# The last 16 pairs of a gated channel mixer as Strassen's seven products, their weight sums made by adding DMA transfers

## The chip, the cores and the metric

The kernel runs on one core of a Trainium2 chip. The metric is the device time of one execution in microseconds (us); the kernel before has a median of 989.22 us over three runs (987.55 to 991.62). The core's engines are TensorE (PE, with its weight loads as PEld), VectorE (DVE), ScalarE (ACT), GpSimd (POOL) and SyncE (SP). SP issues the weight loads; POOL and ACT issue some transfers as well. Tiles in on-chip memory have 128 partitions; matmuls write to PSUM banks of 128 x 512 float32.

## The reference

One block of a streaming encoder, for 512 tokens of 1024 channels. Two token mixers run side by side on the normalised input (a gated delta rule of eight heads, and a convolution with a layer norm); sigmoid gates merge them, an output projection `w_out` adds the result to the input, and then comes the part that the change is about:

```python
h2 = rmsnorm(x, norm2_w[l])
f_gate, f_up = jnp.split(h2 @ ffn_w_gate_up[l], 2, axis=-1)
x = x + (jax.nn.silu(f_gate) * f_up) @ ffn_w_down[l]
return rmsnorm(x, norm_f_w)
```

The hidden width is 2816, that is 22 tiles of 128 columns for the gate and 22 for the up half: 22 pairs.

## The kernel before

Every matmul on weights is done in three terms. `unit` (L92 to L105) loads a weight tile `raw` of 128 x 1024 float32 on SP's queue (512 KB; or two halves of 256 KB), ACT copies it, rounded, to `whi` (L102), and DVE subtracts for the rest, `wlo` (L104); `raw`, `whi` and `wlo` have three buffers each. `split3` (L107 to L113) then issues three matmuls, high weights by high inputs, high by low, low by high. So all these matmuls have the line L113, and the "weight split" of the text is ACT's L102 with DVE's L104.

**Channel mixer** (L873 to L902). For each pair f two column tiles are made, gate and up, each of 8 row blocks by 3 terms: 24 matmuls of 512 columns (all tokens), 48 in a pair. The weights stand still, the normalised tokens `hh`, `hl` move. ACT makes the silu of the gate, DVE the product `fm` (L888). For f below 11, `sums(f)` runs on POOL beside that (L861 to L868): it loads 1 MB of down weights (`wst`), makes four combinations in place (L864 to L867) and stores them (`wsum`, 1 MB). In the second half DVE makes the combinations of the hidden tiles (L898 to L902). `xsplit` (L853, L854) makes high and low parts of an operand, `fh` and `fl`.

**Down product** (from L936). It is already a form of Strassen's method: the hidden tiles are taken as 11 blocks, tokens and columns in halves, and seven products p1 to p7 take the place of eight. `two` runs two products at a time over k = 0 to 10, four banks of PSUM, 12 matmuls of 512 columns for each k; its weights are halves `wd` of the loaded matrix and the stored sums `wsum`. Between them DVE and POOL add the products to the residual `y1` (called A in the trace). p3 comes last (L991 to L1016): six weight tiles, the last three of them first for token block 0, and then for token block 1 in two parts of 256 columns.

**The end.** `norm_f` (L911 to L922) takes each finished part: ACT squares and sums, POOL adds the sums (L796) and raises to the power -1/2 (L798), POOL multiplies the first half of the columns by the norm's weights (L916, to `o0`), ACT scales it (L918), DVE does the second half in one operation (L920, to `o1`), and both halves are stored.

**What sets the order.** The functions are written in order, and a recording layer with a scheduler puts each engine's instructions in a row; each engine works through its row in order and waits for semaphores. So an instruction that waits holds all that stand behind it on its engine. POOL's row also holds the layer norm's sums (L575, `sacc`), for whose end TensorE has a matmul by ones (L580), and the powers of norm 2. In late heads the work is cut into small steps, counted by `count[0]`.

## Time and profile before

| | |
|---|---|
| median of 3 runs | 989.22 us (987.55 to 991.62) |
| the profiled execution's own time | 987.57 us |
| its span (first to last instruction) | 985.8 us |
| matmuls / weight loads | 4775 / 4775 |
| ACT weight copies, 128 x 1024 | 167, mean 1057 ns |
| DVE weight splits, 128 x 1024 | 167, mean 1285 ns |
| loads of gate and up tiles | 44 of 512 KB, 3.4 us to landing |
| DMA traffic | 138.5 MB, mean 140 GB/s |
| read from HBM / written | 119.52 MB / 18.10 MB |

By the chain and the timeline the stages lie as follows: the layer norm's sums on POOL start at 501.7 us, the output products of the two mixers last to 575.6, `w_out` with norm 2 to 635.9, the pairs of the channel mixer to 864.2, the down product to 977.9, the last stores to 985.8.

How rows are read: a row of the timeline has start, duration, engine, line, operation, what is written and read, shape, and how often; in brackets the idle time of the engine before it and what ended that. A row of a group has the busy time and the mean ns of one, then the idle time ahead of the group's instructions. A row of the waits has the total, how many and the longest. A row of the issues has the engine's queue (SPq, POOLq), how many, KB each and the us to landing. Records of matmuls overlap, so that the pace of matmuls is read from their starts.

### The profile page before, as it was taken

The numbers are of one execution on the slowest core, as the hardware profiler recorded it, in microseconds if no ns is written. First come the engines' busy times: TensorE is split into PE (matmuls) and PEld (weight loads), VectorE is DVE, ScalarE is ACT, GpSimd is POOL, SyncE is SP. The second block draws the span as 40 slices with busy tenths as digits, with TensorE's granted clock in tenths as the row PEclk, the third lists the DMA queues.
The fourth block names the chain that finished last, engine by engine and source line by source line (L and its number), as shares of the span: only waits on it lengthen the run. The fifth ranks groups of instructions, "written<-read, shape, count | busy, mean of one in ns | idle before, by whom it ended". The sixth has DMA issues, their size and how long they took to land.

```text
span 985.8 us, 13439 instructions
## 1 busy us (share of the span) xinstructions
PE 955.7 (97%) x4775; PEld 785.7 (80%) x4775; DVE 669.8 (68%) x1044; ACT 513.6 (52%) x1062; POOL 255.1 (26%) x410
## 2 busy tenths in 40 slices
PE   7999999999999999999999999999999999999995
PEld 5688878878787778888878888888888888888784
DVE  4899888888787669889578544542434464469953
ACT  6689777777767664543446323432223322256543
POOL 0314543343243240000050001243534432001412
PEclk9999999999999999999999999999999999999997
DMA  8233421413212122234744432556565565256462
GB/s 317 88 119 120 120 91 41 127 68 98 77 65 88 65 87 69 97 124 144 272 137 137 146 115 65 166 192 246 186 242 206 203 211 184 92 168 196 160 207 86
DMA packets 48291, 138.50 MB, mean 140 GB/s; under 512 B 7472, under 2 KB 9424, under 8 KB 45408
## 3 DMA queue, kind: packets, MB, share of 16 engines
q1 hardware_dynamic: 44016, 112.36, 34.4%
q0 software_dynamic: 3488, 24.17, 6.9%
q10 hardware_dynamic: 720, 1.11, 0.3%
q8 instruction: 37, 0.61, 0.3%
q14 instruction: 30, 0.25, 0.1%
HBM read 119.52 MB, written 18.10 MB: 140 GB/s over the span
## 4 chain that ended last, share of the span: by engine, by line
PE 84%; ACT 5%; DVE 4%; POOL 4%; issue 2%; DMA 1%; SPq 0%; POOLq 0%; ACTq 0%; DVEq 0%
PE mm L113 64%; PE w L113 11%; DVE wlo L104 1%; POOL Un L350 1%; ACT cp L355 1%; ACT Un L349 1%; PE st L477 1%; PE b L415 1%; PE b L421 1%; PE st L483 1%; POOL ytm L376 1%; PE st L489 1%; PE g L346 1%; DMA raw<-in_win_dram 1%; PE st L478 1%
## 5 line engine op out<-in xcount | busy, mean ns | idle before, releaser
L102 ACT ACTIVATE whi<-raw 128x1024 fp32r<-128x1024 f32 x167 | 176.1, 1057 | 327.1 <-PE mm L113 191.9
L113 PE MATMUL mm<-hh,whi 128*128 128x512 f32 x816 | 325.9, 400 | 0.0
L113 PE MATMUL mm<-hl,whi 128*128 128x512 f32 x816 | 321.9, 395 | 2.3 <-POOL hl L229 1.6
L113 PE MATMUL mm<-hh,wlo 128*128 128x512 f32 x816 | 322.3, 395 | 0.0
L104 DVE TENSOR_TENSOR wlo<-raw,whi 128x1024 fp32r<-128x1024 f32 x167 | 214.5, 1285 | 114.7 <-ACT whi L102 114.1
L545 DVE SCALAR_TENSOR_TENSOR cps<-c,c31w,cps 128x512 f32<-128x512 f32 x240 | 180.0, 750 | 4.9 <-ACT cps L543 1.0
L113 PEld LDWEIGHTS mm<-hl,whi 128*128 128x128 f32 x816 | 153.5, 188 | 33.0 <-POOL hl L229 2.9
L113 PEld LDWEIGHTS mm<-hh,wlo 128*128 128x128 f32 x816 | 153.4, 188 | 30.1
L113 PEld LDWEIGHTS mm<-hh,whi 128*128 128x128 f32 x816 | 153.5, 188 | 29.2 <-ACT hh L228 0.2
L888 DVE TENSOR_TENSOR fm<-mm,fsg 128x512 f32<-128x512 f32 x21 | 14.5, 692 | 67.0 <-PE mm L113 67.0
L300 DVE SCALAR_TENSOR_TENSOR acc<-mm,c4w,acc 128x509 f32<-128x509 f32 (+2 forms) x72 | 52.6, 738 | 1.5 <-ACT acc L297 1.2
L376 POOL TENSOR_TENSOR ytm<-U,y 128x60 f32<-128x60 f32 (+14 forms) x120 | 36.9, 307 | 60.6 <-DMA U<-sc 51.9
L113 PE MATMUL mm<-yh,whi 128*128 128x512 f32 x128 | 50.6, 396 | 0.0
L113 PE MATMUL mm<-yh,wlo 128*128 128x512 f32 x128 | 49.8, 389 | 0.0
L113 PE MATMUL mm<-yl,whi 128*128 128x512 f32 x128 | 49.8, 389 | 0.0
L113 PE MATMUL w<-whi,fh 128*128 128x512 f32 (+1 forms) x115 | 45.3, 395 | 2.8 <-ACT whi L102 2.8
L113 PE MATMUL w<-wlo,fh 128*128 128x512 f32 (+1 forms) x115 | 45.6, 397 | 2.4 <-DVE wlo L104 2.4
L113 PE MATMUL w<-whi,fl 128*128 128x512 f32 (+1 forms) x115 | 45.0, 393 | 0.0
L378 POOL TENSOR_TENSOR y<-y,ytm 128x60 f32<-128x60 f32 (+14 forms) x120 | 34.9, 291 | 9.4
L511 POOL TENSOR_TENSOR ss<-ss,half 128x4 f32<-128x4 f32 x8 | 8.1, 1014 | 109.5 <-DVE ss L509 109.5
L796 POOL TENSOR_SCALAR ss<-ss 128x1 f32<-128x1 f32 x17 | 5.7, 338 | 117.9 <-ACT sg L794 105.3
L864 POOL TENSOR_TENSOR wst<-wst 128x512 f32<-128x512 f32 x11 | 15.2, 1386 | 62.7 <-DMA wst<-in_wdn_dram 62.7
(288 smaller groups left out, 1489.1 us busy)
## 6 DMA issues: line engine op xcount, KB each, us to landing
raw<-in_win_dram SPq DMA_DIRECT2D x61, 512.0 KB, 3.3
raw<-in_wgu_dram SPq DMA_DIRECT2D x44, 512.0 KB, 3.4
wst<-in_wdn_dram POOLq DMA_DIRECT2D x11, 1024.0 KB, 5.7
wsum<-wst POOLq DMA_DIRECT2D x11, 1024.0 KB, 4.7
raw<-wsum SPq DMA_DIRECT2D x44, 256.0 KB, 3.2
raw<-in_wdn_dram SPq DMA_DIRECT2D x33, 256.0 KB, 2.9
A<-in_x_dram SPq DMA_DIRECT2D x8, 512.0 KB, 6.3
U<-sc SPq DMA_DIRECT2D x64, 64.0 KB, 2.3
```

The lines of the kernel that those rows point to most:

```text
L102: marked(S.activation(hi[:, 0:n], raw[:, 0:n], AF.Copy), "unit")
L104: marked(V.tensor_tensor(out=lo[:, 0:n], in0=raw[:, 0:n], in1=hi[:, 0:n].bitcast(F32), op=ALU.subtract), "unit")
L113: marked(PE.matmul(ps, l, r, start=first and i == 0, stop=last and i == 2))
L300: marked(V.scalar_tensor_tensor(out=acc[:, s:], in0=ps[:, :T - s], scalar=c4w[:, j, k:k + 1], in1=acc[:, s:], op0=ALU.mult, op1=ALU.add))
L346: PE.matmul(ps[:, n, :], kT[:, n, :], kT[:, n, :], start=True, stop=True)
L349: S.activation(Un[:, n, :], ps[:, n, :], AF.Copy, scale=nb2[:, n:n + 1])
L350: G.tensor_tensor(out=Un, in0=Un, in1=DT, op=ALU.mult)
L376: G.tensor_tensor(out=tm[:, :, 0:w], in0=U[:, k, :, k + 1:], in1=y[:, :, k:k + 1].broadcast_to([P, NT, w]), op=ALU.mult)
L378: last[0] = G.tensor_tensor(out=y[:, :, k + 1:], in0=y[:, :, k + 1:], in1=tm[:, :, 0:w], op=ALU.add)
L545: V.scalar_tensor_tensor(out=acc, in0=c[:, k:k + T], scalar=c31w[:, i, k:k + 1], in1=acc, op0=ALU.mult, op1=ALU.add)
L864: G.tensor_tensor(out=b11, in0=b12, in1=b11, op=ALU.subtract)
L888: V.tensor_tensor(out=fm, in0=pu, in1=sg, op=ALU.mult)
```

## The change

The first six pairs (f = 0 to 5) stay as they are. For each of the last 16, gate and up tile, tokens and rows in halves are taken as a 2 x 2 block product with seven products (`pair`): `hprod` is one of them, 4 row blocks by 3 terms, 12 matmuls of 256 columns (half of the tokens), 84 in a pair. DVE, ACT and PSUM banks combine them to the gate and the up half, and the silu follows. The token sides T1 to T4 of the products are made once, from sums of quarters of `hh` + `hl`. The weight sides are three and a half weight tiles in a pair: a tile `w` as it is, `w46` with half a tile as it is and a sum, `w37` with two sums, `w5` with one.

The sums s1 to s4 of the weights, 16 tiles of 256 KB each, 64 in all, lie in DRAM. `feed_one` makes one: SP copies a part of the gate and up matrix into the tile (behind the weight load just issued, on the same queue), and POOL then issues a transfer that adds another part or another sum (waiting until the copy and, where it takes another sum, that one have landed). One tile is made with each weight tile that is loaded while `start_feed` is set: from count 335 of the heads on, through the output products, the first half of `w_out`, and f = 1 to 9.

The rest follows from the places taken. The down weights' sums are called `dsums`, are written as additions only (signs are taken into the adds of the products) and run on POOL behind every odd pair instead of every early one. The combinations of the hidden tiles and the adds that make p3's operands go from DVE to POOL in part. The residual is stored to DRAM in norm 2 by ACT's queue and loaded back as `y2`, 4 x 512 KB, on SP between the raw halves of the first down product. The load of the last norm's weights moves to the start of the down product. `set_2` to `set_4` are made two k later. At the end, the adds of p4 and p2 and the squares are written between the first k of p3, and POOL's multiply by the norm's weights stays for two of four token blocks; the other two are done by DVE with stores at once.

The core of the diff:

```diff
+        aps = ap if isinstance(ap, tuple) else (ap,)
+        n = T * len(aps) if isinstance(ap, tuple) else 1024
+        raw, hi, lo = ((pool or wp).tile([P, n if pool else 1024], t, name=x)[:, 0:n]
+                       for t, x in ((F32, "raw"), (F32R, "whi"), (F32R, "wlo")))
+        for i, p in enumerate(aps):
+            loads.append(nc.sync.dma_start(raw[:, i * T:(i + 1) * T] if len(aps) > 1 else raw, p))
+        if start_feed[0] and feed:
+            feed_one(last[0])
...
+    FK, F0 = FF // 2, 6
+    sums = {n: dram.tile([FF - F0, P, T], F32, name=n, bufs=1) for n in ("s1", "s2", "s3", "s4")}
+    gu = {n: a["wgu"][r * FF + F0:(r + 1) * FF][:, :, c * T:(c + 1) * T]
+          for n, r, c in (("A11", 0, 0), ("A12", 0, 1), ("A21", 1, 0), ("A22", 1, 1))}
+    feed = [("s1", 0)] + [w for p in range(FF - F0) for w in (("s3", p), ("s2", p), ("s1", p + 1), ("s4", p))]
+    feed = [(*w, *{"s1": ("A21", gu["A22"]), "s3": ("A11", gu["A21"]), "s2": ("A11", sums["s1"]),
+                   "s4": ("A12", sums["s2"])}[w[0]]) for w in feed if w[1] < FF - F0]
+    fed = []
+    def feed_one(behind_):
+        n, p, m, other = feed.pop(0)
+        with tc.issue_after(loads[-1].ins):
+            nc.sync.dma_start(sums[n][p], gu[m][p])
+        with tc.issue_after((fed[-1] if fed else behind_).ins):
+            fed.append(nc.gpsimd.dma_start(sums[n][p], other[p], accum_op=ALU.add, max_dma_last_dim=2048))
...
+        start_feed[0] = count[0] >= 335
...
+            start_feed[0] = not hf
...
+            nc.scalar.dma_start(ysp[n], y1[:, n, :])
...
-        G.tensor_tensor(out=b11, in0=b12, in1=b11, op=ALU.subtract)
-        G.tensor_tensor(out=b12, in0=b22, in1=b12, op=ALU.subtract)
-        G.tensor_tensor(out=b22, in0=b22, in1=b11, op=ALU.subtract)
-        G.tensor_tensor(out=b21, in0=b22, in1=b21, op=ALU.subtract)
+        tt(b22, b12, b22, ALU.add, G)
+        tt(b12, b11, b12, ALU.add, G)
+        tt(b11, b22, b11, ALU.add, G)
+        tt(b21, b11, b21, ALU.add, G)
...
+    def pair(f):
+        z = [bank() for _ in range(4)] if f % 2 == 0 else [bank(), bank2(), bank2(), bank2()]
+        s = lambda n: sums[n][f - F0]
+        w = unit(a["wgu"][f])
+        w46 = unit((a["wgu"][FF + f][:, T:], s("s2")))
+        hprod(z[0][:, t1], w, 0, B11)
+        hprod(z[1][:, t1], w, 1, B21)
+        hprod(z[2][:, t1], w46, 0, T4)
+        w37 = unit((s("s4"), s("s3")))
+        hprod(z[0][:, t2], w46, 1, T2)
+        cw = fq.tile([P, T], F32, name="cw", bufs=2)
+        S.copy(out=cw[:, t1], in_=z[0][:, t1])
+        u = fq.tile([P, TH], F32, name="cu")
+        tt(u, cw[:, t1], z[0][:, t2], ALU.add)
+        hprod(z[1][:, t2], w37, 0, B22)
+        w5 = unit((s("s1"),))
+        hprod(z[3][:, t1], w37, 1, T3)
+        v = fq.tile([P, TH], F32, name="cv2")
+        tt(v, u, z[3][:, t1], ALU.add)
+        if f == F0:
+            xsplit(*T1, b11)
+        hprod(z[2][:, t2], w5, 0, T1)
+        tt(cw[:, t2], u, z[2][:, t2], ALU.add)
+        fm = hidden()
+        tt(fm.rearrange("p (i t) -> p i t", i=2), z[2].rearrange("p (i t) -> p i t", i=2),
+           v.rearrange("p (a t) -> p a t", a=1).broadcast_to([P, 2, TH]), ALU.add)
+        tt(cw, cw, z[1], ALU.add)
+        S.activation(cw, cw, AF.Silu)
+        V.scalar_tensor_tensor(out=fm, in0=fm, scalar=-1.0, in1=cw, op0=ALU.mult, op1=ALU.mult)
...
+        if f % 2 and f // 2 < FK:
+            dsums(f // 2)
+        if f < 2 * F0:
+            operands(f - F0)
+        operands(f)
...
+            if also:
+                with tc.issue_after(loads[-1].ins):
+                    nc.sync.dma_start(*also.pop(0))
             for i in range(2):
                 prods(w, i, xs[k], i, banks[2 * i:2 * i + 2], k == 0, k == FK - 1)
-            then(k)
-
-    def next_set(dst, src):
-        def then(k):
-            dst.append(xset())
-            xsplit(*dst[k], src(k))
-        return then
+            if k > 1:
+                then(k - 2)
...
+        if k < 2:
+            add(2 + k, c1, p4[k])
+            squares(0, 2 + k, c1)
+            squares(1, 2 + k, c2, True)
+        elif k < 4:
+            add(k - 2, c1, p2[k - 2])
+            for cs, eng in ((c1, nc.scalar), (c2, nc.sync)):
+                scaled_out(k, cs, eng)
+            first_half(k - 2)
```

In this diff `tt` is a tensor_tensor on DVE or, with G, on POOL; `bank` and `bank2` give PSUM tiles.

**POOL at the layer norm's sums.** POOL's row before, from the last `ss` of the heads' norms on: `sacc` is the sum over the eight channel tiles, `acc4` the tiles.

```order
L511 TENSOR_TENSOR ss_3642<-ss_3642,half4_83 128x4
L746 DMA nw2_5407<-in_n2w_dram 128x1024
L575 TENSOR_TENSOR sacc_5113<-sacc_5113,acc4_5117 128x512
L575 TENSOR_TENSOR sacc_5113<-sacc_5113,acc4_5121 128x512
L575 TENSOR_TENSOR sacc_5113<-sacc_5113,acc4_5125 128x512
L575 TENSOR_TENSOR sacc_5113<-sacc_5113,acc4_5129 128x512
L575 TENSOR_TENSOR sacc_5113<-sacc_5113,acc4_5133 128x512
L575 TENSOR_TENSOR sacc_5113<-sacc_5113,acc4_5137 128x512
L575 TENSOR_TENSOR sacc_5113<-sacc_5113,acc4_5141 128x512
```

POOL's row of the changed kernel at the same place; `s1` to `s4` are the sums' tiles in DRAM, and a DMA row with `s3<-in_wgu_dram` or `s2<-s1` is the adding transfer's issue.

```order
L160 DMA s3_126<-in_wgu_dram 128x512
L160 DMA s2_125<-s1_124 128x512
L160 DMA s1_124<-in_wgu_dram 128x512
L160 DMA s4_127<-s2_125 128x512
L601 TENSOR_TENSOR sacc_5157<-sacc_5157,acc4_5161 128x512
L601 TENSOR_TENSOR sacc_5157<-sacc_5157,acc4_5165 128x512
L601 TENSOR_TENSOR sacc_5157<-sacc_5157,acc4_5169 128x512
L601 TENSOR_TENSOR sacc_5157<-sacc_5157,acc4_5173 128x512
L160 DMA s3_126<-in_wgu_dram 128x512
L601 TENSOR_TENSOR sacc_5157<-sacc_5157,acc4_5177 128x512
L601 TENSOR_TENSOR sacc_5157<-sacc_5157,acc4_5181 128x512
L601 TENSOR_TENSOR sacc_5157<-sacc_5157,acc4_5185 128x512
```

The seven adds, which stood behind one another, now stand behind the feed's issues, and one issue stands between the fourth and the fifth. (L601 is L575 of before.)

**DVE in the pairs.** DVE's row before, from the second half of f = 10 to the combinations of f = 11, the first late pair; `fm` is a hidden tile, `fl` the low part of an operand, `s1` a combination.

```order
L104 TENSOR_TENSOR wlo_7076<-raw_7072,whi_7074 128x1024
L854 TENSOR_TENSOR fl_6995<-fm_6985,fh_6994 128x256
L104 TENSOR_TENSOR wlo_7108<-raw_7104,whi_7106 128x1024
L888 TENSOR_TENSOR fm_7062<-mm_6999,fsg_7030 128x512
L898 TENSOR_TENSOR s1_7064<-fm_6215,fm_7062 128x256
L104 TENSOR_TENSOR wlo_7148<-raw_7144,whi_7146 128x1024
L854 TENSOR_TENSOR fl_6225<-s1_7064,fh_6224 128x256
L901 TENSOR_TENSOR fm_6215<-fm_6215 128x256
L902 TENSOR_TENSOR fm_6215<-s1_7064,fm_6215 128x256
```

DVE's row of the changed kernel through one Strassen pair (f = 10); `cw`, `cu`, `cv2` are the partial sums out of the banks `w`, L1005 the product with the silu.

```order
L108 TENSOR_TENSOR wlo_7436<-raw_7434,whi_7435 128x1024
L889 TENSOR_TENSOR cu_7370<-cw_7368,w_7296 128x256
L889 TENSOR_TENSOR cv2_7402<-cu_7370,w_7299 128x256
L108 TENSOR_TENSOR wlo_7442<-raw_7440,whi_7441 128x1024
L889 TENSOR_TENSOR cw_7368<-cu_7370,w_7298 128x256
L889 TENSOR_TENSOR fm_7417<-w_7298,cv2_7402 128x512
L889 TENSOR_TENSOR cw_7368<-cw_7368,w_7297 128x512
L108 TENSOR_TENSOR wlo_7485<-raw_7483,whi_7484 128x1024
L1005 SCALAR_TENSOR_TENSOR fm_7417<-fm_7417,cw_7368 128x512
L108 TENSOR_TENSOR wlo_7520<-raw_7518,whi_7519 128x512
L886 TENSOR_TENSOR fl_7427<-fm_7417,fh_7426 128x256
L886 TENSOR_TENSOR fl_7564<-fm_6684,fh_7563 128x256
```

Where a late pair had two splits, `fm` and four short operations, a pair now has four splits (one of half size), five sums out of PSUM, the product and two low parts.

**DVE at the end of the down product.** DVE's row before, with p3's weight splits; A is the residual, `o1` the finished second halves.

```order
L104 TENSOR_TENSOR wlo_8638<-raw_8633,whi_8636 128x1024
L925 TENSOR_TENSOR A_5409<-A_5409,w_8337 128x512
L104 TENSOR_TENSOR wlo_8645<-raw_8640,whi_8643 128x1024
L925 TENSOR_TENSOR A_5409<-A_5409,w_8335 128x512
L925 TENSOR_TENSOR A_5409<-A_5409,w_8336 128x512
L925 TENSOR_TENSOR A_5409<-A_5409,w_8338 128x512
L104 TENSOR_TENSOR wlo_8652<-raw_8647,whi_8650 128x1024
L920 SCALAR_TENSOR_TENSOR o1_8603<-A_5409,ss3_7794,nfw_6152 128x512
L920 SCALAR_TENSOR_TENSOR o1_8622<-A_5409,ss3_7794,nfw_6152 128x512
L104 TENSOR_TENSOR wlo_8659<-raw_8654,whi_8657 128x1024
```

DVE's row of the changed kernel at the same place; `y2` is the reloaded residual.

```order
L108 TENSOR_TENSOR wlo_9748<-raw_9746,whi_9747 128x1024
L889 TENSOR_TENSOR y2_8935<-y2_8935,w_9490 128x512
L889 TENSOR_TENSOR y2_8935<-y2_8935,w_9491 128x512
L108 TENSOR_TENSOR wlo_9755<-raw_9753,whi_9754 128x1024
L889 TENSOR_TENSOR y2_8935<-y2_8935,w_9493 128x512
L1036 SCALAR_TENSOR_TENSOR o1_9815<-y2_8935,ss3_8936,nfw_8933 128x512
L1036 SCALAR_TENSOR_TENSOR o1_9818<-y2_8935,ss3_8936,nfw_8933 128x512
L108 TENSOR_TENSOR wlo_9762<-raw_9760,whi_9761 128x1024
L108 TENSOR_TENSOR wlo_9769<-raw_9767,whi_9768 128x1024
L1036 SCALAR_TENSOR_TENSOR o1_9832<-y2_8935,ss3_8936,nfw_8933 128x512
L108 TENSOR_TENSOR wlo_9776<-raw_9774,whi_9775 128x512
L1036 SCALAR_TENSOR_TENSOR o1_9835<-y2_8935,ss3_8936,nfw_8933 128x512
```

In both, two `o1` stand ahead of the fourth split of p3. Before, they belonged to two token blocks (2 and 3), so that the second waited for the second root factor; now both belong to block 2, and the two of block 3 follow, one behind the fifth split and one behind the sixth.

More of the change, by code (lines that the diff above doesn't have):

```diff
@@ L574, in ln_mean @@
                 S.activation(sq2, cv[i], AF.Square)
[L575 removed]
+                last[0] = G.tensor_tensor(out=vacc, in0=vacc, in1=sq2, op=ALU.add)
         return vacc
@@ L760, in block_kernel @@
         V.tensor_tensor(out=ml[j], in0=mb, in1=mh[j].bitcast(F32), op=ALU.subtract)
+    ysp = [dram.tile([P, D], F32, name="ysp", bufs=NT) for _ in range(NT)]
     def tok_mm(wname, kts, xh, xl, post, between):
@@ new lines, in block_kernel @@
+    kl, kh = slice(0, KH), slice(KH, KD)
+    xb = []
+    for i, (ks, ts, eng) in enumerate(((kl, t1, V), (kl, t2, V), (kh, t2, V), (kh, t1, G))):
+        xb.append(fx.tile([P, KH, TH], F32, name="xb%d" % i))
+        tt(xb[i], hh[:, ks, ts].bitcast(F32), hl[:, ks, ts].bitcast(F32), ALU.add, eng)
+    b11, b12, b22, b21 = xb
+    tt(b11, b11, b12, ALU.subtract)
+    last[0] = tt(b12, b22, b12, ALU.subtract, G)
+    tt(b22, b22, b11, ALU.add)
+    tt(b21, b22, b21, ALU.subtract)
+    T2, T3, T4 = ([fq.tile([P, KH, TH], F32R, name="%s%d" % (n, i)) for n in ("th", "tl")] for i in range(3))
@@ L905, in block_kernel @@
+    fxd = False
+    for f in range(F0, FF):
+        pair(f)
+        if not fxd:
+            fxs.close()
+            ff = ctx.enter_context(tc.tile_pool(name="ff", bufs=FK))
+            fxd = True
+        if f % 2 and f // 2 < FK:
+            dsums(f // 2)
+        if f < 2 * F0:
+            operands(f - F0)
+        operands(f)
+    fqs.close()
     hps.close()
     dp = ctx.enter_context(tc.tile_pool(name="dp", bufs=2, side="right"))
+    nfw = dp.tile([P, D], F32, name="nfw", bufs=1)
@@ L1015, in block_kernel @@
         add(1, cs, ps)
-        norm_f(4 if c else 1, 1, cs)
+        squares(4 if c else 1, 1, cs, c)
+        if not c:
+            out(0)
+    out(1)
 def _layout(i):
```

188 lines of the change are left out of this document (102 added, 86 removed).

## The prediction

> **What bounds the kernel now.** I read the busy shares first, then the chain that ended last, then what TensorE waited for, and then single stretches of the timeline. The page's busy row and its chain row:
>
> ```profile
> PE 955.7 (97%) x4775; PEld 785.7 (80%) x4775; DVE 669.8 (68%) x1044; ACT 513.6 (52%) x1062; POOL 255.1 (26%) x410
> PE 84%; ACT 5%; DVE 4%; POOL 4%; issue 2%; DMA 1%; SPq 0%; POOLq 0%; ACTq 0%; DVEq 0%
> ```
>
> TensorE is busy for 97% of the span, and the chain lies on it for 84%. What is to be had are fewer or shorter matmuls, and its few waits:
>
> ```profile
> PE w L113 <- DVE wlo L104: 2.9, 4, 1.4
> PE w L113 <- ACT whi L102: 2.8, 1, 2.8
> ```
>
> These (total us, times, longest us) are in the down product and at its end. The channel mixer has none: the chain of waits holds one piece of 1007 matmuls.
>
> ```profile
> 635.92 228.28 PE mm L113 x1007
> ```
>
> 228.28 / 1007 = 0.2267 us for a matmul of 512 columns, and 48 of them make a pair of column tiles: 10.88 us.
>
> **Sixteen pairs as seven products: −13.5.** A pair becomes 7 × 12 = 84 matmuls of 256 columns. The kernel has 42 of that form in a row after norm 2; the first and the last:
>
> ```profile
> 623.10 0.28 PE L113 MATMUL w<-hh,whi 128*128 128x256 f32 x1
> 628.00 0.28 PE L113 MATMUL w<-hh,wlo 128*128 128x256 f32 x1
> ```
>
> 41 steps in 4.90 us are 0.1195 us each, so a pair takes 84 × 0.1195 = 10.04 us. It saves 0.84 us, not an eighth of 10.88, because a short matmul is more than half as long as a long one; 16 × 0.84 = 13.5. The Trainium skill (TensorE: Matmul & The Clock Gate, Back-to-back issue gap) gives a lone warm matmul N/2.4 + 2.5 ns, 109 and 216 ns here, by which, as an estimate, a pair would save 1.2 us and sixteen 18.9; both rows here are longer than that, and the rows are used.
>
> **The end of the down product: −6.5 (−2 to −7.3).**
>
> ```profile
> 963.43 0.39 PE L113 MATMUL mm<-wlo,fh 128*128 128x512 f32 x1
> 966.66 0.50 PE L113 MATMUL w<-whi,fh 128*128 128x512 f32 x1 [2.84 <-ACT whi L102]
> 968.74 0.79 PE L113 MATMUL w<-wlo,fh 128*128 128x512 f32 x1 [1.35 <-DVE wlo L104]
> 977.80 0.28 PE L113 MATMUL mm<-wlo,fh 128*128 128x256 f32 x1
> 963.40:974.30 10.90, 6.71 (x21) 4.99 (x20) 4.97 (x6) 5.82 (x11) 2.52 (x6) 0.69 0.25 97
> ```
>
> Behind the matmul at 963.43 stand, in TensorE's order, 15 of 512 columns and 30 of 256: 15 × 0.2267 + 30 × 0.1195 = 7.0 us, so the last could end at 963.66 + 7.0 = 970.65. It starts at 977.80 and ends, by the step, at 977.92: 7.3 us are lost, 4.2 to two waits and the rest to the granted clock, 0.69 in the last row (after the microseconds: busy PE, PEld, DVE, ACT, POOL, then clock). The waits begin on POOL:
>
> ```profile
> 956.16 4.78 POOL L916 TENSOR_TENSOR o<-A,nfw 128x512 f32<-128x512 f32 x3 [23.28 <-DVE A L925]
> 963.57 0.75 DVE L920 SCALAR_TENSOR_TENSOR o<-A,ss,nfw 128x512 f32<-128x512 f32 x1 [5.03 <-POOL ss L798]
> 966.80 0.75 DVE L920 SCALAR_TENSOR_TENSOR o<-A,ss,nfw 128x512 f32<-128x512 f32 x1 [2.48 <-POOL ss L798]
> 962.60 0.28 POOL L796 TENSOR_SCALAR ss<-ss 128x1 f32<-128x1 f32 x1
> 962.97 0.57 POOL L798 TENSOR_TENSOR ss<-ss,half 128x1 f32<-128x1 f32 x1
> ```
>
> Four multiplies by the norm's weights stand ahead of the two root factors on POOL, the DVE's two output multiplies wait for these, and a weight split waits behind them. The change leaves POOL two such multiplies, one of them behind the first factor. From 956.2 that gives a multiply of 1.6 (4.78 / 3), two sums and a power (2 × 0.28 + 0.57), so the first factor at 959.4. The two DVE multiplies ahead of the fourth split now both want that factor alone: with 2 × 0.75 and the split's 1.22 it ends at 962.1, and the third matmul behind 963.66 wants it at 964.1. Nothing is late next by this; another multiply and a slow step on ACT would eat the 2 us and leave up to 1 or so: I take −6.5. If some other wait takes most of it, 2 is what the one spared POOL multiply (1.6) with its clock should still bring. The steps behind the last matmul stay as they are.
>
> **DVE beside POOL in the pairs: +4 (0 to +5.8).** A pair now asks this of DVE: three splits and a half one, five operations of 256 columns, two of 512 out of PSUM, and a multiply.
>
> ```profile
> 669.31 1.22 DVE L104 TENSOR_TENSOR wlo<-raw,whi 128x1024 fp32r<-128x1024 f32 x1 [0.15 <-ACT whi L102]
> 657.59 0.69 DVE L888 TENSOR_TENSOR fm<-mm,fsg 128x512 f32<-128x512 f32 x1 [3.37 <-PE mm L113]
> 756.23 0.42 DVE L898 TENSOR_TENSOR s<-fm 128x256 f32<-128x256 f32 x1
> ```
>
> With the 0.75 of the output multiply above, 3 × 1.22 + 0.69 + 5 × 0.42 + 2 × 0.69 + 0.75 = 8.6 us of 10.04: covered, with 1.5 us of room. A late pair of before asks for two splits, one product and four short ones, 2 × 1.22 + 0.69 + 4 × 0.42 = 4.8 of 10.88. POOL takes from it, as the stretch with six POOL sums on end shows:
>
> ```profile
> 925.50 7.38 POOL L925 TENSOR_TENSOR A<-A,v 128x512 f32<-128x512 f32 x4
> 927.99 2.31 DVE L104 TENSOR_TENSOR wlo<-raw,whi 128x1024 fp32r<-128x1024 f32 x1
> 930.22 1.51 DVE L854 TENSOR_TENSOR fl<-fm,fh 128x256 fp32r<-128x256 f32 x1
> 930.35 0.50 PE L113 MATMUL w<-wlo,fh 128*128 128x512 f32 x1 [0.42 <-DVE wlo L104]
> 934.02 0.50 PE L113 MATMUL w<-wlo,fh 128*128 128x512 f32 x1 [0.65 <-DVE wlo L104]
> ```
>
> A split beside a POOL sum takes 2.31 for 1.22, a 256-column one 1.51 for 0.42: 1.09 lost each time. There the whole burst cost TensorE 0.42 + 0.65 = 1.07 us, 0.18 for each POOL sum. Eight groups of down sums (32 POOL sums of 512 columns) fall behind f = 7 to 21: 32 × 0.18 = 5.8 by these rows, and nothing if the room holds. The burst is denser than the pairs will be; I take 4. The 22 combinations of 256 columns that POOL takes from DVE relieve it by as much as they hold it, and count nothing.
>
> **Making the gate and up sums: +5 (0 to +22).** Each of 64 sums is a copy of 256 KB on SP's queue behind a weight load, then an adding transfer on POOL's. No such transfer is in this trace; the nearest rows are plain ones.
>
> ```profile
> raw<-in_wgu_dram SPq DMA_DIRECT2D x44, 512.0 KB, 3.4
> wst<-in_wdn_dram POOLq DMA_DIRECT2D x11, 1024.0 KB, 5.7
> wsum<-wst POOLq DMA_DIRECT2D x11, 1024.0 KB, 4.7
> 700.00:740.00 40.00, 40.00 (x178) 33.14 (x177) 13.63 (x15) 11.27 (x16) 14.90 (x13) 1.00 0.64 226
> GB/s 317 88 119 120 120 91 41 127 68 98 77 65 88 65 87 69 97 124 144 272 137 137 146 115 65 166 192 246 186 242 206 203 211 184 92 168 196 160 207 86
> ```
>
> 226 GB/s at a share of 0.64 are 353 at full share (an estimate); the highest slice had 317. The first 49 tiles go beside heads, output products and f = 1 to 5, where a weight tile (0.52 MB) with copy and addition (0.52) takes over 5 us: some 200 GB/s, free. The last 15 fall into f = 6 to 9 with two groups of down sums. There SP must bring 3.5 weight tiles and four copies in each 10.04 us, 1.84 + 1.05 = 2.88 MB or 287 GB/s, 10.8 MB over 3.75 pairs; POOL's queue adds 15 × 0.26 + 2 × 2.1 = 8.1 MB. If all of it goes through in that stage, 18.9 MB at 317 GB/s need 60 us for 37.7: +22. But these tiles are wanted twelve pairs later and the down sums not before the down product, so POOL may lag; only SP's loads must be in time, and 287 fit into 317. I take 5, nearer the low end, for loads that land late now and then.
>
> **Smaller terms: +1.9.** (a) One adding transfer stands between the fourth and the fifth sum of the layer norm on POOL, for whose last sum TensorE waits today without room:
>
> ```profile
> 663.39 0.57 POOL L868 DMA_DIRECT2D wsum<-wst  x1 [0.30 <-POOL wst L867]
> 514.64 1.08 PE L580 MATMUL mm<-sacc,cst 128*128 128x512 f32 x2
>   POOL sacc L575: 0.2, 1
> ```
>
> An issue is 0.57 us: +0.6 (0 to +2, if its copy has not landed). (b) The token sums add nine 1024-wide operations to DVE's row and two to POOL's, between norm 2's last transposes and f = 2, where a pair leaves DVE 6 us of room (4.8 of 10.88 used, above); one of them waits for a POOL sum that stands behind the first down sums, with weight splits queued behind it: +0.8 (0 to +2). (c) Four reloads of the residual, 512 KB each, go ahead of raw halves in the first down product: +0.5 (0 to +1.5). The signs that moved, the later load of the last norm's weights and the lagging operand sets cost nothing: same operations, off the chain, TensorE's row order kept.
>
> **The sum.** −13.5 − 6.5 + 4 + 5 + 1.9 = −9.1. The profiled execution took 987.57 us (span 985.8 and 1.8 around it), 1.65 under the median of 989.22: 987.57 − 9.1 = 978.5, and as a median 980.1.
>
> **Rivals.** *A, on the other side: the queues share.* If the additions and down sums take half of the DMA engines in f = 6 to 9 whenever they have work, SP's loads fall behind by the whole excess, +22 for my +5: 980.1 + 17 = 997.1, slower by over 0.5%. It decides once POOL's queue never runs dry there; from +19.1 on it is slower. For it: 18.9 MB, against 353 × 37.7 = 13.3 that fit. Against it: POOL issues one addition per copy landed, so its queue empties itself. The Trainium skill (DMA: Bandwidth & Descriptors, Queues, rings and completion order) says that each engine goes round the queues that have work; by that rule A holds as long as POOL's queue has any; no row here shows the two queues at odds.
>
> *B: DVE becomes the bound.* If every one of the 32 POOL sums holds an operation for 1.09, 2.3 in each of the 14 pairs from f = 8, DVE needs 8.6 + 2.3 × 1.09 = 11.1 us for 10.04: 14 × 1.06 = +15 for my +4, 991.1. For it: the stretch at 925. Against it: one beside which a DVE operation out of PSUM ran lost nothing,
>
> ```profile
> 744.12 1.30 POOL L864 TENSOR_TENSOR wst<-wst 128x512 f32<-128x512 f32 x1 [7.05 <-DMA wst<-in_wdn_dram]
> 744.63 0.69 DVE L888 TENSOR_TENSOR fm<-mm,fsg 128x512 f32<-128x512 f32 x1 [3.37 <-PE mm L113]
> ```
>
> and five of DVE's eleven or so in a pair read PSUM.
>
> *C: all is hidden.* −13.5 − 7.3 and no costs: 987.57 − 20.8 + 1.65 = 968.4. For it: no wait in the channel mixer today.
>
> *D: the end stays as it is.* Another wait takes the place of POOL's, as two output multiplies still stand ahead of the fourth split on DVE: 980.1 + 6.5 = 986.6. For it: that order; against it: POOL's row above, which shows what the wait was made of. That the new pairs are not shorter at all would need the loads of weights to pace them; a load is 188 ns,
>
> ```profile
> L113 PEld LDWEIGHTS mm<-hl,whi 128*128 128x128 f32 x816 | 153.5, 188 | 33.0 <-POOL hl L229 2.9
> ```
>
> yet the 42 short matmuls step at 0.1195 with such loads between them, so I give this nothing of its own.
>
> **Chances.** Forecast 0.55 (974 to 985 on its own, mostly by the 4 and the 5), A 0.16, B 0.11, C 0.11, D 0.07. About 0.5%, 4.9 us, is what a measurement of this kernel tells from no change: faster is under 984.3, slower over 994.2. Faster takes C and the forecast but 0.03: 0.63. Same takes B, D and that 0.03: 0.21. Slower is A: 0.16. The range runs from C to B with the bounds of the terms, 968 to 993; A is left out.
>
> **What would show it.** Right: the new pairs step at about 10.05 us from f = 10 on and TensorE's rows in the last ten microseconds follow one another at clock 1. Wrong: waits for raw loads at f = 6 to 9 with DMA share 1.0 (A); waits for the low halves in every odd pair, with 2.3 us splits (B); a wait for the fourth split at the end (D). A time above 994 or below 968 refutes the sum.

## The result, and the profile after

The changed kernel takes 1053.57 us (median of 4 runs, 1049.71 to 1057.42), the kernel before 988.62 (4 runs): a ratio of 1.065, 95% interval 1.061 to 1.070. It is slower by 65 us where 9 less were forecast. The profiled execution took 1053.38 us, its span is 1051.6.

The page of the changed kernel, its busy shares, its chain and the software queue of its DMA engines (packets, MB, share of 16 engines):

```profile
PE 960.0 (91%) x5351; PEld 814.2 (77%) x5351; DVE 745.8 (71%) x1135; ACT 546.3 (52%) x1112; POOL 342.0 (33%) x507
q0 software_dynamic: 12704, 40.95, 16.2%
PE 67%; DMA 10%; POOL 6%; DVE 6%; ACT 5%; issue 4%; SPq 1%; POOLq 0%; ACTq 0%; DVEq 0%
```

TensorE's busy time hardly changed (960.0 for 955.7), yet its share fell from 97% to 91%, and the chain lies on transfers for 10% where it was 1%. So the time came as waits. TensorE's waits in the changed kernel (us in total, times, longest):

```profile
PE w L117 <- ACT whi L107: 45.9, 7, 36.8
PE w L117 <- DVE wlo L108: 8.1, 11, 1.3
PE mm L117 <- ACT whi L107: 6.5, 3, 3.0
PE mm L117 <- DVE wlo L108: 4.2, 6, 0.9
```

One wait is 36.8 us long. Where the pairs lie is seen best from ACT, which makes one silu (L1004) near the end of each of the 16 Strassen pairs; the rows of f = 6, 12, 13, 15 and 21:

```profile
712.27 0.61 ACT L1004 ACTIVATE cw<-cw 128x512 f32<-128x512 f32 x1
800.65 0.61 ACT L1004 ACTIVATE cw<-cw 128x512 f32<-128x512 f32 x1
850.79 0.63 ACT L1004 ACTIVATE cw<-cw 128x512 f32<-128x512 f32 x1 [3.72 <-DVE cw L889]
872.76 0.63 ACT L1004 ACTIVATE cw<-cw 128x512 f32<-128x512 f32 x1 [1.12 <-DVE cw L889]
933.04 0.63 ACT L1004 ACTIVATE cw<-cw 128x512 f32<-128x512 f32 x1 [1.44 <-DVE cw L889]
```

Six pairs from f = 6 to 12 take 88.4 us (14.7 each), the pair f = 13 alone 50.1, the last six from f = 15 on 60.3, 10.05 each. So the products themselves run at the forecast pace of 10.04, from f = 15 on. Ahead of f = 15 there are two losses in the changed kernel, and its windows tell them apart (us, busy PE, PEld, DVE, ACT, POOL, then TensorE's clock, DMA share, GB/s):

```profile
740.00:780.00 40.00, 32.14 (x231) 30.62 (x231) 25.30 (x35) 13.62 (x23) 16.40 (x16) 0.91 0.91 273
780.00:820.00 40.00, 23.44 (x166) 22.44 (x164) 15.72 (x20) 8.05 (x11) 19.72 (x18) 0.80 0.75 233
805.00:845.00 40.00, 3.17 (x28) 2.96 (x26) 1.27 (x4) 1.44 (x3) 16.44 (x17) 0.58 0.43 159
820.00:860.00 40.00, 12.70 (x87) 11.79 (x87) 14.34 (x16) 7.25 (x11) 21.52 (x21) 0.64 0.49 175
860.00:900.00 40.00, 40.00 (x333) 40.00 (x334) 32.85 (x51) 19.91 (x28) 6.17 (x8) 1.00 0.61 191
```

From 740 to 780 the DMA engines are nearly full (0.91) and TensorE works for four fifths of the time. From 805 to 845 they are more than half idle (0.43), TensorE, ACT and DVE all but stand still, and only POOL is busy: that is no lack of transfers but a queue at POOL. Once POOL is through, at 860, all is as forecast.

The long wait, followed backwards through the engines: the matmul, ACT's operand part, DVE's combination `s` (s1 in the code), and POOL's combinations.

```profile
844.97 0.58 PE L117 MATMUL w<-hh,whi 128*128 128x256 f32 x1 [36.83 <-ACT whi L107]
843.56 0.42 ACT L885 ACTIVATE fh<-s 128x256 fp32r<-128x256 f32 x1 [41.77 <-DVE s L889]
843.10 0.42 DVE L889 TENSOR_TENSOR s<-fm 128x256 f32<-128x256 f32 x1 [37.73 <-POOL fm L889]
631.42 0.88 POOL L921 DMA_DIRECT2D wst<-in_wdn_dram  x1
837.35 0.55 POOL L927 DMA_DIRECT2D wsum<-wst  x1 [0.30 <-POOL wst L889]
837.92 0.73 POOL L889 TENSOR_TENSOR fm<-fm 128x256 f32<-128x256 f32 x1
842.33 0.73 POOL L889 TENSOR_TENSOR fm<-s,fm 128x256 f32<-128x256 f32 x1
```

DVE wants to write s1 of f = 12 into the one buffer that there is; POOL has not yet read s1 of f = 11 out of it, because its combinations of f = 11 stand behind ten groups of down sums, of which the first begins at 631 and the tenth is stored at 837. DVE stands, ACT stands behind DVE's s1 with the next weight copy in its row, and TensorE behind ACT.

The end of the down product is as it was hoped for: the last matmul starts at 1042.86, and the twelve microseconds up to 1042 have no wait and run at full clock.

```profile
1030.00:1042.00 12.00, 12.00 (x65) 10.37 (x64) 8.83 (x11) 6.22 (x15) 8.04 (x11) 1.00 0.37 135
1042.86 0.28 PE L117 MATMUL mm<-wlo,fh 128*128 128x256 f32 x1
```

### The profile page after: what moved, and what is told of

Read it like the earlier page. It is cut to its first block, busy times and chain, and to the rows that moved or that the text cites. A ratio compares the mean times of both kernels' runs of the same rounds, so it can differ in the third digit from the quotient of the medians.

```text
span 1051.6 us, 15190 instructions
## 1 busy us (share of the span) xinstructions
PE 960.0 (91%) x5351; PEld 814.2 (77%) x5351; DVE 745.8 (71%) x1135; ACT 546.3 (52%) x1112; POOL 342.0 (33%) x507
## 3 DMA queue, kind: packets, MB, share of 16 engines
q0 software_dynamic: 12704, 40.95, 16.2%
## 4 chain that ended last, share of the span: by engine, by line
PE 67%; DMA 10%; POOL 6%; DVE 6%; ACT 5%; issue 4%; SPq 1%; POOLq 0%; ACTq 0%; DVEq 0%
PE mm L117 45%; PE w L117 14%; DMA raw<-s 4%; DVE wlo L108 3%; DMA wst<-in_wdn_dram 2%; POOL wst L889 2%; ACT whi L107 2%; POOL Un L376 1%; DMA wsum<-wst 1%; DMA raw<-wsum 1%; ACT cp L381 1%; ACT Un L375 1%; PE b L441 1%; PE st L503 1%; PE b L447 1%
## 5 line engine op out<-in xcount | busy, mean ns | idle before, releaser
L108 DVE TENSOR_TENSOR wlo<-raw,whi 128x1024 fp32r<-128x1024 f32 x199 | 255.6, 1286 | 124.4 <-ACT whi L107 116.3
L117 PE MATMUL mm<-hh,whi 128*128 128x512 f32 (+1 forms) x656 | 254.9, 389 | 2.7 <-ACT whi L107 2.7
L117 PE MATMUL mm<-hh,wlo 128*128 128x512 f32 (+1 forms) x656 | 251.5, 383 | 2.7 <-DVE wlo L108 2.7
L117 PE MATMUL mm<-hl,whi 128*128 128x512 f32 (+1 forms) x656 | 250.6, 382 | 2.3 <-POOL hl L255 1.6
L117 PEld LDWEIGHTS mm<-hh,wlo 128*128 128x128 f32 x656 | 125.0, 191 | 24.1 <-DVE wlo L108 3.7
L117 PE MATMUL w<-hh,whi 128*128 128x256 f32 x192 | 56.4, 295 | 41.0 <-ACT whi L107 40.8
L889 POOL TENSOR_TENSOR wst<-wst 128x512 f32<-128x512 f32 x44 | 69.0, 1567 | 56.8 <-DMA wst<-in_wdn_dram 54.6
L117 PEld LDWEIGHTS w<-hh,whi 128*128 128x128 f32 x192 | 38.1, 199 | 42.4 <-ACT whi L107 41.8
L117 PE MATMUL w<-hh,wlo 128*128 128x256 f32 x192 | 56.7, 296 | 5.5 <-DVE wlo L108 5.3
L117 PE MATMUL w<-hl,whi 128*128 128x256 f32 x192 | 55.5, 290 | 1.0 <-DVE hl L859 1.0
```

The source lines that it names most:

```text
L108: marked(V.tensor_tensor(out=lo, in0=raw, in1=hi.bitcast(F32), op=ALU.subtract), "unit")
L117: marked(PE.matmul(ps, l, r, start=first and i == 0, stop=last and i == 2))
L889: return eng.tensor_tensor(out=out, in0=in0, in1=in1, op=op)
```

## The experiments

Three causes are to be told apart. **R**: POOL's row, which hands the lateness of the down sums on to DVE through s1. **D**: the DMA engines, filled by the adding transfers and the down sums. **H**: POOL's adds hold DVE's operations (rival B). **T** stands for the transfers of the down sums alone. Each run is compared with runs of the kernel before on the same chip (medians of 988.2 to 989.9). The runs without one kind of sum or both are there for the time alone; they leave work out.

**1. Six buffers for s1.**

```diff
-        s1 = fq.tile([P, TH], F32, name="s1")
+        s1 = fq.tile([P, TH], F32, name="s1", bufs=6)
```

> The combinations' short tile s1 gets six buffers in place of one, so that DVE's next s1 need not wait until POOL has read the last one. Theory R (POOL's row: the combinations of f = 11 stand behind ten groups of down sums and all adding transfers, and the single buffer hands that lateness to DVE, ACT and TensorE): the wait of 36.8 us at 845 goes, so 1053.6 - 37 = 1017, within 5, and the pairs of f = 6 to 12 stay at 12 to 16 us each. Theory D (the DMA engines are too full in the channel mixer and everything is late because of that): the wait turns into waits for loads, and the time stays over 1040.

1020.66 us (ratio 1.031, 1.027 to 1.035): 32.9 less than the changed kernel. TensorE's longest wait for ACT is now 3.4 us:

```profile
PE w L117 <- ACT whi L107: 9.7, 6, 3.4
```

The pairs of f = 7 to 12 still take 12.8 to 16.5 us. R is right for 33 us; the other 31 above the kernel before have another cause.

**2. Down sums tied behind the combinations.**

```diff
-        nc.gpsimd.dma_start(r, a["wdn"][k].rearrange("p (i c) -> p i c", i=4))
+        with tc.issue_after(last[0].ins):
+            nc.gpsimd.dma_start(r, a["wdn"][k].rearrange("p (i c) -> p i c", i=4))
```

> Each group of down sums is tied behind the last combination written before it on POOL, so that groups 6 to 10 run after the combinations of f = 12, 14, 16, 18 and 20 and not before that of f = 11. Theory R: the combination of f = 11 is reached before the next s1 wants it, the wait of 36.8 us goes, 1017, within 5; a little less (1010) if fewer transfers of down sums in f = 8 to 12 help the loads there. Theory D: over 1040, with the loss moved to later pairs.

1022.15 us (1.033, 1.031 to 1.035), at the edge of what was expected. That is 31 us by another way, through POOL's order in place of memory: it is the order on POOL that matters, not something about the buffer. One new wait of 9.0 us stands at 918.7 in the down product; its cause was not followed. The pairs from f = 14 to 21 now take 9 to 15 us in turn, as the later groups run beside them: the loss of a group goes where the group goes.

**3. No feed.** The 64 weight sums are left out; the pairs load plain quarters of the matrix.

```diff
     fed = []
+    feed = []
...
-        s = lambda n: sums[n][f - F0]
+        s = lambda n: a["wgu"][FF + f if n in ("s1", "s3") else f][:, (T if n in ("s3", "s4") else 0):][:, 0:T]
```

> The 64 weight sums of gate and up are left out: no copies, no adding transfers; the pairs load plain quarters of the matrix in their place (same sizes, same matmuls). Theory R + D (two causes, one after the other): the pairs of f = 6 to 12 run at 10.1 us, about 38 us back, but the ten groups of down sums still stand ahead of the first combination: from 631 at 15 us each they end near 785, f = 12 comes to its s1 at 765, so some 15 to 25 us of waiting stay: 1053.6 - 38 - 15 = 1000, within 10. Theory D alone: no wait is left, 1053.6 - 75 = 979 or less. Theory R alone: as the kernel, less POOL's waits for copies, 1030 to 1050.

1024.44 us (1.034, 1.032 to 1.036), 24 over what was expected. The long wait is still there, 31.1 us; and the pairs of f = 7 to 12 take 11.7 to 13.4 us without a single adding transfer. So the down sums slow the short pairs by themselves; the expectation, which gave all of that to the feed, was wrong.

**4. No down sums.** The eleven groups are left out; the down product loads plain parts.

```diff
     def dsums(k):
+        return
...
-    wt = lambda k, i: wsum[k][:, {1: 1, 2: 0, 3: 3, 4: 2}[i], :]
+    wt = lambda k, i: wd(k, {1: 1, 2: 0, 3: 3, 4: 2}[i])
```

> The eleven groups of down sums are left out (the down product loads plain parts in their place). Theory R + D: POOL reaches the combinations in time, so the 36.8 us go, and with 23 MB less in the pairs at least half of the 38 us of f = 6 to 12 too: 1053.6 - 37 - 19 to 38 = 978 to 998. Theory D with the adding transfers as its cause: the 38 us stay, 1015.

984.19 us (0.994, 0.992 to 0.996). The feed alone slows only f = 7 and 8 (12.8 and 14.2 us); with its end the pairs are back at 10.1. Its windows:

```profile
700.00:740.00 40.00, 36.90 (x295) 35.49 (x295) 24.67 (x38) 18.26 (x27) 8.15 (x10) 1.00 1.01 280
740.00:780.00 40.00, 40.00 (x336) 40.00 (x335) 32.12 (x50) 20.57 (x31) 3.07 (x4) 1.00 0.61 197
```

The DMA engines are full in the first, at 280 GB/s, and TensorE loses 3 us there. The chain has two loads of sums (`raw<-s`) of 7.3 and 10.0 us in that window, where the median of such a load in this run is 3.5.

**5. Transfers of the down sums alone** (no feed, as in run 3, six buffers for s1, and POOL's 44 adds left out).

```diff
-        tt(b22, b12, b22, ALU.add, G)
-        tt(b12, b11, b12, ALU.add, G)
-        tt(b11, b22, b11, ALU.add, G)
-        tt(b21, b11, b21, ALU.add, G)
```

> As the run without the feed (the 64 weight sums of gate and up left out, plain quarters loaded), with six buffers for s1, and of the down sums only the loads and stores stay: POOL's 44 adds are left out. So the only down-sum work in the pairs is 23 MB of transfers. Theory H (the adds on POOL hold DVE's operations and slow the short pairs from 10.1 to some 12.5 us): the pairs go back to 10.1 to 10.5 us, 972 to 980. Theory T (the 1 MB transfers delay the weight loads): the pairs stay at 11.5 to 13 us while groups run, 985 to 995.

983.28 us (0.994, 0.991 to 0.996): between the two expectations. The pairs stay at 11 to 12.8 us while groups are moved, as T has it, but the groups are through sooner, at 766. The six groups loaded from 690 on cost some 7 us beside run 6, 1.2 each.

**6. No sums of either kind** (runs 3 and 4 together, with six buffers).

> Both kinds of sums left out: no feed, no down sums, plain parts loaded in their places. What is left is what the seven products and the new end bring by themselves. By the forecast's terms 989.5 - 13.5 - 6.5 + 1.9 = 971.4, within 3. If the new pairs or the end hide another loss: 975 or more.

975.95 us (0.987, 0.984 to 0.991): what the seven products and the new end bring by themselves. The short pairs take 10.08 us on average:

```profile
705.68 0.63 ACT L1006 ACTIVATE cw<-cw 128x512 f32<-128x512 f32 x1 [1.43 <-DVE cw L890]
856.93 0.63 ACT L1006 ACTIVATE cw<-cw 128x512 f32<-128x512 f32 x1 [1.44 <-DVE cw L890]
862.70 2.81 SPq L1067 DMA_DIRECT2D y<-ysp  x4
874.29 0.50 PE L117 MATMUL w<-whi,fh 128*128 128x512 f32 x1 [3.48 <-ACT whi L107]
```

856.93 - 705.68 is 15 times 10.08. It misses 971.4 by 4.5 and so falls under the second case; the last two rows show most of why: the four reloads of the residual come together, SP's row waits about 1 us for the memory that they go to, and the next weight half takes 7.6 us to land behind them (a piece of the chain). TensorE waits 3.5 us for it and then runs a stretch at low clock (0.72 from 876 to 880).

**7. Eleven long and eleven Strassen pairs**, all down sums beside the long ones.

```diff
-    FK, F0 = FF // 2, 6
+    FK, F0 = FF // 2, 11
...
-    fs = ctx.enter_context(tc.tile_pool(name="fs", bufs=1))
     fxs = ctx.enter_context(ExitStack())
+    fs = fxs.enter_context(tc.tile_pool(name="fs", bufs=2))
...
-        if f % 2:
-            dsums(f // 2)
+        for k in range(f * FK // F0, (f + 1) * FK // F0):
+            dsums(k)
```

(and no groups in the second loop, and six buffers for s1)

> All sums are made, but beside the long pairs: eleven long pairs, eleven Strassen pairs, so 44 weight sums, all fed before f = 5; one group of down sums written with each long pair, two buffers for them (memory that the operands take later), six buffers for s1. Theory R + H + T together (sums in the short pairs are what costs): short pairs at 10.1 us, 989.5 - 11 x 0.8 - 6.5 + 3 = 977, within 4. If the slow pairs have another cause in Strassen's form itself: 990 or more.

1006.45 us (1.017, 1.014 to 1.019). The short pairs are all at 10.1 us, so the form itself is sound, but two other waits came. One is at the token sums, of which POOL makes two, behind down sums:

```profile
670.39 2.27 DVE L889 TENSOR_TENSOR xb<-xb,xb 128x1024 f32<-128x1024 f32 x1 [13.22 <-POOL xb L889]
772.08 0.42 ACT L885 ACTIVATE fh<-fm 128x256 fp32r<-128x256 f32 x1 [16.27 <-DMA wsum<-wst]
773.50 0.58 PE L117 MATMUL mm<-hh,whi 128*128 128x256 f32 x1 [10.31 <-ACT whi L107]
```

DVE stands for 13.2 us there, and TensorE for 5.4 and 2.5 (at 675 and 679). The other, in the last two rows, is at the first short pair: ACT waits with an operand for the memory of the down sums, which the operands take over, and TensorE waits 10.3 behind it.

**8. Eight long and fourteen Strassen pairs**, feed from count 240 on; otherwise as run 7.

```diff
-    FK, F0 = FF // 2, 6
+    FK, F0 = FF // 2, 8
...
-        start_feed[0] = count[0] >= 335
+        start_feed[0] = count[0] >= 240
```

> The same with eight long and fourteen Strassen pairs; 56 weight sums, the feed from count 240 of the heads on so that it ends before the pairs; the eleven groups of down sums written into the eight long pairs. By the same theory 989.5 - 14 x 0.8 - 6.5 + 3 = 975 if the groups end with f = 7 (some 90 us for eleven at 8 each), up to 985 if they run on into the short pairs at 15 us each. More than 990 if POOL's waits in the heads delay their chains.

1018.82 us (1.029, 1.026 to 1.033), over the first two cases, and not for the reason of the third: the groups are not through at f = 8 (the last store is issued at 767), and the pair f = 9 takes 37 us, 23.6 of them in one wait behind an operand.

**9. No feed, all down sums, six buffers** (run 3 with the edit of run 1).

> The run without the feed once more (the 64 weight sums of gate and up left out), now with six buffers for s1 and all down sums made, adds and transfers. Beside the run with the transfers alone (983.3) it gives the price of POOL's 44 adds among the short pairs. Theory H (the adds hold DVE's operations): 983 + 8 to 14 = 991 to 997, with low-part operations of 1.8 and 2.3 us beside the adds. If only the transfers cost: 983 to 986.

1002.37 us (1.014, 1.013 to 1.016), over the range of H: beside run 5 the 44 adds cost 19.1 us. How, in one pair of this run:

```profile
731.87 6.67 POOL L890 TENSOR_TENSOR wst<-wst 128x512 f32<-128x512 f32 x4 [6.37 <-DMA wst<-in_wdn_dram]
732.50 1.78 DVE L1006 SCALAR_TENSOR_TENSOR fm<-fm,cw 128x512 f32<-128x512 f32 x1
734.20 1.78 DVE L108 TENSOR_TENSOR wlo<-raw,whi 128x512 fp32r<-128x512 f32 x1
735.90 2.92 DVE L887 TENSOR_TENSOR fl<-fm,fh 128x256 fp32r<-128x256 f32 x2
740.01 0.38 PE L117 MATMUL w<-hh,wlo 128*128 128x256 f32 x1 [2.29 <-DVE wlo L108]
744.52 0.69 DVE L1006 SCALAR_TENSOR_TENSOR fm<-fm,cw 128x512 f32<-128x512 f32 x1
```

Beside POOL's four adds DVE's product takes 1.78 us, and 0.69 a pair later without them; the half split and the two low parts lose as much each (0.69 and 0.42 without). Four of these, one after the other, are 4.3 us, where DVE had 1.5 us of room, and TensorE waits 2.3. The adds also stretch a group from 13 to 19 us, so that eight and not six fall among the short pairs; at 1.2 us for a group's transfers some 2.4 of the 19.1 are due to that (an estimate from run 5).

**10. Run 7 with its three waits mended**: token sums all on DVE behind the product of f = 1, three buffers for the down sums, reloads at k = 3, 5, 7 and 9.

```diff
-    for i, (ks, ts, eng) in enumerate(((kl, t1, V), (kl, t2, V), (kh, t2, V), (kh, t1, G))):
+    for i, (ks, ts, eng) in enumerate(((kl, t1, V), (kl, t2, V), (kh, t2, V), (kh, t1, V))):
...
-            if also:
+            if also and k > 2 and k % 2:
```

> Eleven long and eleven Strassen pairs as before in this study, and the three waits seen there mended: the token sums all on DVE and behind the product of f = 1, three buffers for the down sums so that they end before the short pairs, the residual's reloads at k = 3, 5, 7 and 9 of the first down product. From 1006: the waits of 10.3 and 5.4 us at the token sums and some 11 us at the first short pair go, and 3 to 5 at the start of the down product: 989.9 - 8.8 - 6.5 + 1 = 976, within 4. If POOL's row finds another wait to pass on: over 985.

991.53 us (1.003, 1.002 to 1.005): 15 us better, and 15 short of what was expected. The list of waits in the expectation has the 10.3 us twice, once at the token sums and once as the "some 11 us" at the first short pair; counted once, it leads from 1006 to about 987 and not to 976. The token sums on DVE now meet POOL's adds (three operations in a row take 6.8 us, 1.2 each without the adds), and TensorE waits 2.5 us there. For the layer norm's sums it waits 1.6 us: they begin 3.9 us later than before, of which 2 come from heads that were late already.

**11. The same with eight long pairs**, feed from count 240 on.

> The same with eight long and fourteen Strassen pairs and the feed from count 240. If the eleven groups end before the first short pair (some 90 us at three buffers): 989.9 - 11.2 - 6.5 + 2 = 974, within 4. If they run on into the short pairs: 980 to 1000, with the loss in the first two or three of them.

1000.26 us (1.012, 1.010 to 1.014), at the upper end of the second case expected. The groups run on into f = 8 (the last stores are issued at 742), and near 749 TensorE waits 11.5 us for a split that stands on DVE behind an operand, which waits for those groups' memory.

**12. Run 10 with the losses spread**: each adding transfer one weight load later, token sums one or two for each of f = 2 to 9, the first short pair's operands one pair later, reloads at k = 6 to 9.

```diff
-        with tc.issue_after((fed[-1] if fed else behind_).ins):
-            fed.append(nc.gpsimd.dma_start(sums[n][p], other[p], accum_op=ALU.add, max_dma_last_dim=2048))
+        owed.append((n, p, other))
+        if len(owed) > 1:
+            pay(behind_)
...
-            if also and k > 2 and k % 2:
+            if also and k > 5:
```

> The run with eleven long and eleven Strassen pairs once more, against four losses that its trace shows: the layer norm's sums on POOL began 3.9 us late behind an adding transfer that waited for its copy (each adding transfer is now issued one weight load later, when its copy has landed); the token sums met POOL's adds in f = 1 (now one or two for each of f = 2 to 9); the operands of the first short pair waited some 4 us for memory of the down sums (now made one pair later); the residual's reloads held SP's row (now at k = 6 to 9). From 991.5: -3 -3 -4 -2 = 979, within 4, and faster than the kernel before by about 1%. If POOL's adds in the long pairs cost what is left: 985 to 990.

985.92 us (12 runs; before 988.22, 17 runs; 0.997, 0.995 to 0.999). It is well ahead of the changed kernel, but ahead of the kernel before by some 0.3% only, too little to call it faster, and it lies at the lower edge of its second expectation. Eleven short pairs and the new end should bring 11 x 0.80 + 7.3 = 16 us and bring 2.3. The profiled execution, 3.8 us shorter than that of the kernel before, shows where most of the other 12 go. From 636 to 750, through the long pairs, TensorE works without a gap at full clock. At the first short pair ACT once more waits with an operand for the memory of the down sums, and TensorE behind it:

```profile
753.05 0.42 ACT L895 ACTIVATE fh<-fm 128x256 fp32r<-128x256 f32 x1 [9.15 <-DMA wsum<-wst]
754.47 0.38 PE L119 MATMUL mm<-hh,whi 128*128 128x256 f32 x1 [3.20 <-ACT whi L109]
```

With a second wait of 0.8 us and a granted clock of 0.73 from 750.4 to 763, some 7 us are lost there. Down product and end take 118.4 us for 121.6 before, 4 short of the 7.3.

## Why the prediction was wrong

Laid one upon the other, the runs lead from the kernel without sums to the changed one, median by median. The differences add up by construction; each is known to some 3 us, as wide as the intervals of runs 5 and 6 are to either side.

| step | us | adds |
|---|---|---|
| products and new end, no sums (run 6) | 976.0 | |
| with the transfers of the down sums (run 5) | 983.3 | +7.3 |
| with POOL's adds too (run 9) | 1002.4 | +19.1 |
| with the feed too (run 1) | 1020.7 | +18.3 |
| with one buffer for s1 (the changed kernel) | 1053.6 | +32.9 |

(The feed alone, run 4 against run 6, is +8.2, so another order of the steps would share the sum out otherwise.) The forecast's terms beside that:

**The pairs, -13.5: right.** 10.08 us for a pair against 10.88, 16 x 0.80 = -12.8.

**The end, -6.5: right.** No wait at the end and full clock, so that all of the 7.3 us came back. What stood against it came from a small term, below. (A slip without weight: by its own rows the first root factor comes at 958.9 and not at 959.4.)

**"The 22 combinations ... that POOL takes from DVE relieve it by as much as they hold it, and count nothing": this step failed, and it is the largest error.** It counted their duration and not their place. In POOL's row of the changed kernel ten groups of down sums and all adding transfers stand ahead of the first combination; the prediction put eight groups "behind f = 7 to 21", as the code is written, and let POOL lag because its sums are wanted late. The combinations stood in the same row and were wanted soon. Run 1 (memory) and run 2 (order) each give back 31 to 33 us, of a wait of 36.8. It was none of the rivals. It does not carry the wrong sign alone: without it, in run 1, the kernel is still 31 us slower than the one before, through the next two terms.

**"DVE beside POOL in the pairs: +4 (0 to +5.8)": mechanism right, size wrong.** 19.1 us (run 9 against run 5), some 2.4 of them for two groups more among the short pairs. The price of 0.18 us for an add came from one burst in the down product; by run 9 an add costs 19.1 / 44 = 0.43, and more than that if one counts only the 32 that fall among short pairs. The 1.09 us that an operation loses were right, and rival B's +15 for the stage was nearer than the term itself. The Trainium skill (SBUF — State Buffer, Who interferes with whom) says that a DVE instruction with two inputs from SBUF contends with a GpSimd instruction that reads SBUF, and that one with at most one such input, outside the modes with two ports, does not. The trace agrees: in run 9 the product and the half split, with two inputs from SBUF, go from 0.69 to 1.78 us beside the adds, while the product that reads PSUM, in the prediction's row at 744.63, kept its 0.69 beside one.

**"Making the gate and up sums: +5 (0 to +22)": wrong in size and place.** The feed alone is 8.2, the down sums' transfers 7.3, and in company with the adds the feed is 18.3, so that transfers of both kinds come to 25.6, if nothing of the 18.3 is DVE's. Rival A, with +22, was near that amount, in part by luck, for it counted four pairs only. The argument against it failed: POOL's queue did not empty itself, because the adding transfers stood on POOL behind the down sums. The last copy was issued on SP's queue at 731, the last addition at 796, through f = 12 and not f = 9. The Trainium skill (DMA: Bandwidth & Descriptors, Queues, rings and completion order) lets each DMA engine go round the queues that have work. The full engines and late loads of run 4's first window are what that would give; how the engines were shared no run shows.

**The smaller terms, +1.9: about 7.5.** The end of f = 5 came at 693.4 (a piece of the chain that starts at 649.96 and lasts 43.40 us) for 635.92 + 5 x 10.88 = 690.3 before, 3.0 later. Of that, 1.0 was there before the layer norm's second sums began: the matmul by ones ahead of them came at 498.42 for 497.43, and the one behind them at 515.65 for 514.64. So (a) cost nothing, and 2.1 are left for (b), put at 0.8 with 2 as the upper end. (c), the reloads, were put at 0.5 with 1.5 as the upper end and are 5.4: a wait of 3.5 us in run 6 (3.95 in the changed kernel), and 63 matmuls behind it in 16.2 us for 14.3. (The first row is of the kernel before, the others of the changed one.)

```profile
497.43 1.02 PE L564 MATMUL mm<-sacc,cst 128*128 128x512 f32 x2
498.42 1.02 PE L590 MATMUL mm<-sacc,cst 128*128 128x512 f32 x2
515.65 1.02 PE L606 MATMUL mm<-sacc,cst 128*128 128x512 f32 x2
649.96 43.40 PE mm L117 x190
950.88 0.68 PE L117 MATMUL w<-whi,fh 128*128 128x512 f32 x1 [3.95 <-ACT whi L107]
```

What stays open is how the 18.3 us of the feed among all sums divide between full DMA engines and DVE's shorter room; only the sum and the single parts were measured.

## What to carry to other kernels

An operation that is moved to another engine is to be looked up in that engine's row: everything between it and what stands there now is its wait, and everything that waits for it inherits that, through a single buffer as much as through data. "It may lag" holds for an engine only when it holds for each instruction in its row. And the price of a contention is not that of the place where it was measured: 0.18 us an add in one burst of the down product became 0.43 and more among pairs that leave DVE 1.5 us in 10, so the room of the stage has to be part of the sum.

## What the runs showed of the hardware

The adding transfers are costly for the DMA engines. Before, the software queue moved 24.17 MB in 6.9% of 985.8 us:

```profile
q0 software_dynamic: 3488, 24.17, 6.9%
```

That is 68 us of all sixteen engines, 2.8 us for 1 MB. After, it is 40.95 MB in 16.2% of 1051.6 us, 170 us; the 16.8 MB of the 64 adding transfers took the other 102, 6.1 us for 1 MB or 1.6 us for each 256 KB tile, more than twice as much by the byte. Runs 4 and 6, both without down sums, differ by the feed alone. The hardware and the software queue of run 4, then of run 6:

```profile
q1 hardware_dynamic: 63024, 143.83, 43.6%
q0 software_dynamic: 9536, 17.88, 11.2%
q1 hardware_dynamic: 53808, 127.05, 40.2%
q0 software_dynamic: 320, 1.10, 0.4%
```

By the spans of 982.5 and 973.7 us the 64 copies on SP's queue took 37 us of all sixteen engines, 2.2 us for 1 MB, and the 64 adding transfers 106 us, 6.3 us for 1 MB, with as many bytes and packets each (16.8 MB, 9216). So it is not the size of the packets; whether it is the adding, or the software queue with such packets, no run separates.

POOL's issue of one lasts 0.80 to 1.19 us in the changed kernel's trace (median 0.81 and 0.83 for the two kinds of source) where a plain one takes 0.6 on average.
